# One split per FFN weight tile on ACT and DVE, and one sum of the seven products by an adding transfer

## The chip, the core and the metric

The kernel runs on one core of one Trainium2 chip. A core has five engines that each work through their own queue in order and wait for each other by semaphores: PE multiplies matrices, DVE and ACT work elementwise, POOL does small elementwise work and issues transfers, and SP issues transfers. The metric is the device time of one execution in microseconds. The time before is 1067.16 us, the median of three runs from 1063.83 to 1067.43.

## What is computed

One decoder layer for 256 tokens and 16 meta tokens with 2048 channels, in float32. After attention, pooling and a first normalisation comes the part that the change touches, a gated FFN with a causal convolution of width 3, and a second normalisation:

```python
def conv_gated_ffn(h, w_up, conv_w, conv_b, w_down):
    T = h.shape[1]
    z = h @ w_up
    zp = jnp.pad(z, ((0, 0), (CONV_WIDTH - 1, 0), (0, 0)))
    z = sum(zp[:, j:j + T] * conv_w[j] for j in range(CONV_WIDTH)) + conv_b
    a, g = jnp.split(z, 2, axis=-1)
    return (jax.nn.gelu(a) * g) @ w_down
...
        f = conv_gated_ffn(h, w_up[l], conv_w[l], conv_b[l], w_down[l])
        h = layer_norm(ALPHA * h + f, ln2_g[l], ln2_b[l])
```

`w_up` is 2048 by 11264, `w_down` 5632 by 2048.

## The kernel before

**Two parts for each number.** PE multiplies rounded float32 values (fp32r). To keep float32 precision, each operand is split into a high part (the value rounded) and a low part (the rest), and each product is three matmuls: high by high, high by low, low by high (L172 to L174 in `product`, L742 to L744 in `seven`). For weights the split is made on the chip as they arrive, in `fetch`: SP issues the transfer of a 128 x 2048 tile into a raw buffer `wraw` (L108), ACT copies it to the high half of `whl` (L121), and DVE writes raw minus high into the low half (L122). Raw and split buffers both come three deep, so a transfer waits until the L122 of three tiles earlier has ended, and a split waits until PE has done with the tile three earlier. `weights()` asks for a tile, and with it for the next two.

**Up tiles and down tiles.** An up tile is one block of 128 output channels of `w_up`: 48 matmuls of 258 columns. Its result goes through the convolution on ACT and DVE (L680 to L682), and for each second up tile the gate (L697, L698). Two gated blocks make a pair, which is turned into the left-hand forms of a seven-product scheme for 2 x 2 blocks: sums on POOL (`forms`, L717 to L720), their high and low parts on ACT and DVE (`two_parts`, L703 and L704).

A down tile holds the four blocks b11, b12, b21, b22 of 512 columns that belong to one pair and one half c of the output. Of kind A, it serves four products (P2, P3, P1, P5), after DVE has put b12 - b11 in the place of b12 (L113). Of kind B, it serves three (P7, P6, P4), after DVE has made three differences and sums in place (L116, L117, L118, which write b12, b11 and b21 in this order); then only 1536 columns are split. The products of one part and one half c are summed over the part's pairs in PSUM; four pairs (three in parts of 6) make an A phase, and then as many tiles of kind B a B phase.

**The order.** The 44 channel blocks come in parts of 8, 8, 8, 8, 6 and 6 (`PARTS`). `ffn_plan` lays the up tiles of one part between the down tiles of the part before it, in even shares: one to one as long as the parts are equal, four down tiles to three up tiles while the fifth part goes up and the fourth comes down. The last part's down projection is done plainly at the end. The first four blocks (`FOLDED`) are multiplied before the first normalisation is known, and put right afterwards by `unfold`; these are the first eight up tiles. The order on each engine is not that of the source: a scheduler in the framework arranges the instructions of all engines from its own estimate of their times when the kernel is built.

**The sums.** At the end of an A phase ACT copies P1 and P5 to `u` and `v` (L754, L756), DVE adds P2 and P3 to the output blocks c11 and c12 in `y2` (`add`, L750), and POOL issues two transfers that add `u` to c11 and `v` to c12 in place (L759, L760). At the end of a B phase DVE adds `v` (still P5) to c22, `u` becomes P1 + P6 (L764), `v` becomes `u` + P7 (L765), P4 goes to c21, and three more adding transfers bring `u` to c12 and `v` to c21 and c22. In the first part `add` also multiplies the block by ALPHA.

The two lines that say how a tile is cut:

```python
        cuts = (0, 1024, 2048)
...
            cuts = (0, 1024, 1536)
```

Of the kernel before, what the change touches and what calls it, by code (L numbers as in the profile page):

```python
# [14 lines left out]
ALU = mybir.AluOpType  # L15
# [53 lines left out]
def tile_layer(ctx, tc, xt, w_first, w_proj, w_uk, w_uv, w_pool, w_o, w_up, w_down, cols, rows, rel_bias, onehot, out):  # L69
    nc = tc.nc  # L70
# [10 lines left out]
    def small():  # L81
        return pa.tile([P, 512], F32, tag="at", name="at")
# [9 lines left out]
    stream = [w_proj[j] for j in range(8)] + [w_uk, w_uv] + [w_proj[j] for j in range(8, 24)]  # L92
    stream += [w_o[j] for j in range(KT)]
    plan = ffn_plan()
    kinds = {}
    for item in plan:
        if item[0] == "up":
            stream.append(w_up[item[2] * FT + item[1]])
        else:
            kinds[len(stream)] = item[0]  # L100
            stream.append(w_down[sum(PARTS[:item[1]]) + item[2] * (PARTS[item[1]] // 2) + item[3]])
    stream += [w_down[d] for d in range(FT - PARTS[-1], FT)]
    spare, scattered = len(stream) - PARTS[-1], (len(stream) - 2, len(stream) - 1)
# [3 lines left out]
    def fetch(raw, hl, src, kind=None):  # L107
        nc.sync.dma_start(raw, src)  # L108
        b11, b12, b21, b22 = (raw[:, c:c + 512] for c in range(0, 2048, 512))
        cuts = (0, 1024, 2048)  # L110
        if kind == "A":

            nc.vector.tensor_tensor(b12, b12, b11, op=ALU.subtract)  # L113
        if kind == "B":

            nc.vector.tensor_tensor(b12, b22, b12, op=ALU.subtract)  # L116
            nc.vector.tensor_tensor(b11, b12, b11, op=ALU.add)  # L117
            nc.vector.tensor_tensor(b21, b21, b11, op=ALU.subtract)  # L118
            cuts = (0, 1024, 1536)
        for c in (slice(a, b) for a, b in zip(cuts, cuts[1:])):  # L120
            nc.scalar.activation(hl[:, 0, c], raw[:, c], AF.Copy)  # L121
            nc.vector.tensor_tensor(hl[:, 1, c], raw[:, c], hl[:, 0, c].bitcast(F32), op=ALU.subtract)  # L122
# [4 lines left out]
    def emit(i):  # L127
        if i in ready:
            return
        if i in scattered:  # L130

            raw = wp.tile([P, 2048], F32, tag="wraw", name="wraw")
            nc.sync.dma_start(raw, stream[i])
            ready[i] = []
            for c in range(0, 2048, 256):
                hl = ring.tile([P, 2, 256], F32R, tag="act", name="whl_r", padded_shape=[P, 2, T])
                nc.scalar.activation(hl[:, 0, :], raw[:, c:c + 256], AF.Copy)
                nc.vector.tensor_tensor(hl[:, 1, :], raw[:, c:c + 256], hl[:, 0, :].bitcast(F32), op=ALU.subtract)
                ready[i].append(hl)
            return  # L140
        if i == spare:
            raw = wp.tile([P, 2048], F32, tag="wraw", name="wraw")
            hl = sb.tile([P, 2, 2048], F32R, tag="y", name="whl_y")
        else:
            raw, hl = weight_tiles()
        fetch(raw, hl, stream[i], kinds.get(i))
        ready[i] = hl
# [6 lines left out]
    def weights(ahead=2):  # L154
        i = state["use"]
        state["use"] += 1
        prefetch(i + 1 + ahead)
        return ready.pop(i)
# [113 lines left out]
    cuts = ((0, P), (P, 2 * P), (2 * P, T))  # L272
    v = sb.tile([P, 3], F32, name="rms_v")
# [103 lines left out]
    for i, (a, b) in enumerate(((0, NM), (NM, NM + P), (NM + P, T))):  # L377
        if i:
            v = ap_.tile([b - a, 1024], F32, name=f"v{i}")
        else:  # L380

            v = ap_.tile([80, 1024], F32R, name="v0")
# [248 lines left out]
    cuts = ((0, P), (P, 2 * P), (2 * P, NQ))  # L631
# [68 lines left out]
    held = {}  # L700
# [30 lines left out]
    def seven(kind, part, c, j):  # L731

        hl = weights()
        n = PARTS[part] // 2
        names = (("P2", 2), ("P3", 3), ("P1", 0), ("P5", 1)) if kind == "A" else (("P7", 1), ("P6", 0), ("P4", 2))
        if j == 0:
            for name, _ in names:
                held[name] = small()
        for name, w in names:
            a, i = pairs[part][j][name]  # L740
            ps, w = held[name], slice(512 * w, 512 * w + 512)
            nc.tensor.matmul(ps, a[:, 0, i], hl[:, 0, w], start=j == 0, stop=False)  # L742
            nc.tensor.matmul(ps, a[:, 0, i], hl[:, 1, w], start=False, stop=False)  # L743
            nc.tensor.matmul(ps, a[:, 1, i], hl[:, 0, w], start=False, stop=j == n - 1)  # L744
        if j < n - 1:
            return
        c11, c12, c21, c22 = (y2[:, i, w:w + 512] for i in range(2) for w in (512 * c, 1024 + 512 * c))

        def add(to, ps):
            nc.vector.scalar_tensor_tensor(to, to, 1.0 if part else ALPHA, ps, op0=ALU.mult, op1=ALU.add)  # L750

        if kind == "A":
            held["u"] = fp.tile([P, 512], F32, name="u", tag="u1", bufs=1, padded_shape=[P, 2 * NQ])
            nc.scalar.activation(held["u"], held["P1"], AF.Copy)  # L754
            held["v"] = fp.tile([P, 512], F32, name="v", tag="u2", bufs=1, padded_shape=[P, 2 * NQ])
            nc.scalar.activation(held["v"], held["P5"], AF.Copy)  # L756
            add(c11, held["P2"])
            add(c12, held["P3"])
            nc.gpsimd.dma_start(c11, held["u"], accum_op=ALU.add)  # L759
            nc.gpsimd.dma_start(c12, held["v"], accum_op=ALU.add)  # L760
        else:
            u, v = held["u"], held["v"]
            add(c22, v)
            nc.vector.tensor_tensor(u, u, held["P6"], op=ALU.add)  # L764
            nc.vector.tensor_tensor(v, u, held["P7"], op=ALU.add)  # L765
            add(c21, held["P4"])
            nc.gpsimd.dma_start(c12, u, accum_op=ALU.add)
            nc.gpsimd.dma_start(c21, v, accum_op=ALU.add)
            nc.gpsimd.dma_start(c22, v, accum_op=ALU.add)
# [4 lines left out]
    for item in plan:  # L774
        if item[0] in "AB":
            seven(*item)
            continue
        _, f, half_ = item
        part = next(p for p in range(len(PARTS)) if f < sum(PARTS[:p + 1]))
# [161 lines left out]
```

## Time and profile before

| | us |
|---|---|
| median of three runs | 1067.16 |
| lowest, highest | 1063.83, 1067.43 |
| the profiled execution | 1061.57 |
| its span, first to last instruction | 1059.8 |

How to read the rows. A page row of an engine gives its busy time, its share of the span and its instructions. PE's weight loads (PEld) overlap its matmuls, and matmuls overlap each other, so the pace of PE is read from starts. A row of stretches gives the stretch, its length and each engine's busy time in it with the number of instructions, then the clock that PE was granted, the mean busy share of the 16 DMA engines, and GB/s. A row of waits gives who waited for whom, the total in us, the times and the longest. A row of a group gives line, engine, operation, out<-in, shapes and count, then busy us and the mean ns of one, then the idle time of the engine just before them and what ended it. A row of the timeline gives start and length in us, the engine, line and operation, and x4 where four equal ones follow each other. Line numbers are those of the kernel before.

### The profile page before, as it was taken

How to read it: one execution, taken by the hardware profiler on the slowest of the kernel's cores; microseconds unless marked ns; L12 is line 12 of the kernel's file. 1: busy time of each engine (PE TensorE's matmuls, PEld its weight loads, DVE VectorE, ACT ScalarE, POOL GpSimd, SP SyncE). 2: the span in 40 equal slices, each digit the busy share in tenths (PEclk: the TensorE clock that was granted, in tenths of full speed). 3: DMA queues.
4: the chain of work that ended last, by engine and by line, in shares of the span. 5: the costliest groups of instructions: out<-in, count | busy, mean ns of one | idle time of the engine just before them, and what ended most of it. 6: DMA issues, size and time to landing. Idle time of an engine off the chain costs nothing. (4 is left out here: it accounts for less than half of the span.)

```text
span 1059.8 us, 19247 instructions
## 1 busy us (share of the span) xinstructions
PE 1040.1 (98%) x7683; PEld 989.0 (93%) x7683; DVE 902.1 (85%) x1391; ACT 605.1 (57%) x968; POOL 207.0 (20%) x257
## 2 busy tenths in 40 slices
PE   9999999999999999999999999999999998999996
PEld 8998999999999999999999999999999897999985
DVE  6879468848769987899899989899898999998977
ACT  6566445745447765565565656565565555665650
POOL 1100014125345321210112101122011212200020
PEclk9999999999999999999999999999999999999998
DMA  8756542454552577898787797877878787898882
GB/s 319 255 172 238 192 148 96 158 184 168 181 190 93 187 228 233 276 292 279 270 292 271 267 298 268 280 262 273 296 272 271 260 288 262 286 300 300 298 272 80
DMA packets 60330, 253.16 MB, mean 239 GB/s; under 512 B 21798, under 2 KB 22224, under 8 KB 32976
## 3 DMA queue, kind: packets, MB, share of 16 engines
q1 hardware_dynamic: 34448, 231.86, 60.3%
q0 software_dynamic: 8320, 16.93, 8.4%
q10 hardware_dynamic: 17472, 3.15, 1.6%
q8 instruction: 60, 0.98, 0.4%
q14 instruction: 30, 0.25, 0.1%
HBM read 234.60 MB, written 2.11 MB: 223 GB/s over the span
## 5 line engine op out<-in xcount | busy, mean ns | idle before, releaser
L122 DVE TENSOR_TENSOR whl<-wraw,whl 128x1024 fp32r<-128x1024 f32 (+1 forms) x418 | 491.0, 1210 | 53.2 <-ACT whl L121 51.1
L121 ACT ACTIVATE whl<-wraw 128x1024 fp32r<-128x1024 f32 (+1 forms) x418 | 403.5, 1012 | 133.9 <-DVE wraw L113 28.9
L172 PE MATMUL mm<-hp,whl 128*128 128x258 f32 x1280 | 364.6, 285 | 0.2 <-ACT whl L121 0.2
L174 PE MATMUL mm<-hp,whl 128*128 128x258 f32 x1280 | 361.9, 283 | 1.5 <-DVE whl L122 1.5
L173 PE MATMUL mm<-hp,whl 128*128 128x258 f32 x1280 | 362.6, 283 | 0.0
L173 PEld LDWEIGHTS mm<-hp,whl 128*128 128x128 f32 x1280 | 244.3, 191 | 3.1
L174 PEld LDWEIGHTS mm<-hp,whl 128*128 128x128 f32 x1280 | 243.8, 190 | 1.9 <-DVE whl L122 1.9
L172 PEld LDWEIGHTS mm<-hp,whl 128*128 128x128 f32 x1280 | 242.1, 189 | 3.5 <-ACT whl L121 0.4
L172 PE MATMUL mm<-xp,whl 128*128 128x256 f32 (+5 forms) x384 | 111.0, 289 | 0.0
L173 PE MATMUL mm<-xp,whl 128*128 128x256 f32 (+5 forms) x384 | 109.5, 285 | 0.0
L174 PE MATMUL mm<-xp,whl 128*128 128x256 f32 (+5 forms) x384 | 109.1, 284 | 0.3 <-DVE whl L122 0.3
L742 PE MATMUL at<-whl,gp 128*128 128x512 f32 x190 | 75.2, 396 | 0.0
L743 PE MATMUL at<-whl,gp 128*128 128x512 f32 x190 | 74.9, 394 | 0.0
L744 PE MATMUL at<-whl,gp 128*128 128x512 f32 x190 | 74.8, 394 | 0.0
L172 PEld LDWEIGHTS mm<-xp,whl 128*128 128x128 f32 x384 | 72.7, 189 | 0.6
L174 PEld LDWEIGHTS mm<-xp,whl 128*128 128x128 f32 x384 | 72.5, 189 | 0.8 <-DVE whl L122 0.8
L173 PEld LDWEIGHTS mm<-xp,whl 128*128 128x128 f32 x384 | 72.3, 188 | 0.8 <-issue 0.5
L680 ACT ACTIVATE z<-mm,cv 128x256 f32<-128x256 f32 x40 | 22.5, 561 | 79.0 <-PE mm L174 78.1
L720 POOL TENSOR_TENSOR forms<-za 128x128 f32<-128x128 f32 x19 | 18.4, 967 | 207.4 <-DVE za L698 199.9
L680 ACT ACTIVATE za<-mm,cv 128x256 f32<-128x256 f32 x40 | 22.5, 562 | 56.1 <-PE mm L174 56.1
L717 POOL TENSOR_TENSOR forms<-za 128x128 f32<-128x128 f32 x19 | 21.5, 1130 | 126.4 <-DVE za L698 126.3
L744 PEld LDWEIGHTS at<-whl,gp 128*128 128x128 f32 x190 | 35.7, 188 | 8.6
(299 smaller groups left out, 1927.5 us busy)
## 6 DMA issues: line engine op xcount, KB each, us to landing
wraw<-in_w_up SPq DMA_DIRECT2D x88, 1024.0 KB, 5.3
wraw<-in_w_down SPq DMA_DIRECT2D x82, 1024.0 KB, 6.1
wraw<-in_w_proj SPq DMA_DIRECT2D x24, 1024.0 KB, 4.9
wraw<-in_w_o SPq DMA_DIRECT2D x16, 1024.0 KB, 4.8
y<-v POOLq DMA_DIRECT2D x30, 256.0 KB, 8.4
y<-u POOLq DMA_DIRECT2D x20, 256.0 KB, 4.4
wraw<-in_w_first SPq DMA_DIRECT2D x9, 304.0 KB, 5.5
x<-in_xt SPq DMA_DIRECT2D x1, 2176.0 KB, 8.4
```

The source lines that it names most:

```text
L121: nc.scalar.activation(hl[:, 0, c], raw[:, c], AF.Copy)
L122: nc.vector.tensor_tensor(hl[:, 1, c], raw[:, c], hl[:, 0, c].bitcast(F32), op=ALU.subtract)
L172: nc.tensor.matmul(ps, wh, ah, start=n == 0, stop=False)
L173: nc.tensor.matmul(ps, wh, al, start=False, stop=False)
L174: nc.tensor.matmul(ps, wl, ah, start=False, stop=n == KT - 1)
L680: nc.scalar.activation(z, src[:, 2:NQ], AF.Identity, bias=col(C_B, j), scale=col(C_W, 3 * j + 2))
L717: nc.gpsimd.tensor_tensor(s[:, 0], a21, a22, op=ALU.add)
L720: nc.gpsimd.tensor_tensor(s[:, 3], a11, a21, op=ALU.subtract)
L742: nc.tensor.matmul(ps, a[:, 0, i], hl[:, 0, w], start=j == 0, stop=False)
L743: nc.tensor.matmul(ps, a[:, 0, i], hl[:, 1, w], start=False, stop=False)
L744: nc.tensor.matmul(ps, a[:, 1, i], hl[:, 0, w], start=False, stop=j == n - 1)
```

## The change

`kinds` now also holds the up tiles, under "up", so that `fetch` sees a kind for every tile of the FFN but the last six. With a kind, a tile is cut in one piece: 2048 columns for up tiles and kind A, 1536 for kind B. Tiles without a kind (the projections, `w_o`, and the last six of `w_down`) keep their two pieces. Further, in all parts but the first, the addition of P5 to c22 moves from DVE at the end of the B phase to an adding transfer from `v` that POOL issues at the end of the A phase.

```diff
@@ -94,10 +94,10 @@
     for item in plan:
+        kinds[len(stream)] = item[0]
         if item[0] == "up":
             stream.append(w_up[item[2] * FT + item[1]])
         else:
-            kinds[len(stream)] = item[0]
             stream.append(w_down[sum(PARTS[:item[1]]) + item[2] * (PARTS[item[1]] // 2) + item[3]])
@@ -107,7 +107,7 @@
-        cuts = (0, 1024, 2048)
+        cuts = (0, 2048) if kind else (0, 1024, 2048)
         if kind == "A":
@@ -116,7 +116,7 @@
             nc.vector.tensor_tensor(b21, b21, b11, op=ALU.subtract)
-            cuts = (0, 1024, 1536)
+            cuts = (0, 1536)
@@ -758,9 +758,12 @@
             nc.gpsimd.dma_start(c11, held["u"], accum_op=ALU.add)
             nc.gpsimd.dma_start(c12, held["v"], accum_op=ALU.add)
+            if part:
+                nc.gpsimd.dma_start(c22, held["v"], accum_op=ALU.add)
         else:
             u, v = held["u"], held["v"]
-            add(c22, v)
+            if part == 0:
+                add(c22, v)
```

## The prediction

> **What bounds the kernel now.** I read the page's busy shares first, then the stretches by stage, then who waited for whom on PE.
>
> ```profile
> span 1059.8 us, 19247 instructions
> PE 1040.1 (98%) x7683; PEld 989.0 (93%) x7683; DVE 902.1 (85%) x1391; ACT 605.1 (57%) x968; POOL 207.0 (20%) x257
> ```
> ```profile
> core 0: us, PE busy (x) PEld busy (x) DVE busy (x) ACT busy (x) POOL busy (x), PEclk, DMA share, GB/s
> 283.00:412.00 129.00, 127.33 (x1046) 125.79 (x1046) 110.52 (x187) 79.19 (x132) 47.02 (x49) 1.00 0.55 180
> 412.00:570.00 158.00, 158.00 (x1121) 148.93 (x1120) 142.78 (x193) 93.17 (x129) 24.46 (x30) 1.00 0.85 279
> 570.00:821.00 251.00, 251.00 (x1774) 236.34 (x1773) 227.40 (x314) 149.31 (x208) 42.88 (x51) 1.00 0.81 275
> 821.00:915.00 94.00, 90.45 (x616) 83.23 (x615) 86.71 (x118) 53.75 (x74) 16.14 (x16) 1.00 0.81 269
> 915.00:1012.00 97.00, 97.00 (x696) 91.79 (x695) 91.71 (x126) 58.80 (x81) 10.99 (x13) 1.00 0.89 298
> ```
> ```profile
> PE mm L174 <- DVE whl L122: 2.2, 4, 0.8
> PE at L742 <- ACT whl L121: 2.0, 1, 2.0
> PE at L743 <- DVE whl L122: 0.8, 1, 0.8
> ```
> The FFN runs from 283 to 1012. TensorE sets its pace: it is busy for the whole of three of the five stretches, at a granted clock of 1.00. It loses 129 - 127.33 = 1.67 us while the first tiles run on unnormalised input, and 94 - 90.45 = 3.55 us in 821:915, where each up tile meets more down tiles. So 5.2 us is nearly all that any relief of DVE or ACT can give back here, and 0.5% of the time (5.3 us, about what a measurement can tell from no change) is as much. DVE is close behind PE: 227.40 of 251 us (91%), 86.71 of 94 (92%). The question is not how much work is taken off DVE and ACT but whether each tile is still ready when PE comes for it.
>
> **The change part by part: the pieces.** Durations by form, then one pair of tiles (an up tile and a kind-B down tile) on DVE, PE and ACT:
>
> ```profile
> L122 DVE TENSOR_TENSOR whl<-wraw,whl 128x1024 fp32r<-128x1024 f32 x380 | 468.6, 1262 | 53.2 <-ACT whl L121 51.1 <-PE at L485 0.8 <-PE at L530 0.8
> L121 ACT ACTIVATE whl<-wraw 128x1024 fp32r<-128x1024 f32 x380 | 384.8, 1051 | 133.9 <-DVE wraw L113 28.9 <-DVE wraw L117 27.5 <-issue 26.5
> L121 ACT ACTIVATE whl<-wraw 128x512 fp32r<-128x512 f32 x38 | 23.4, 616 | 0.0
> L750 DVE SCALAR_TENSOR_TENSOR y<-y,v 128x512 f32<-128x512 f32 x10 | 7.0, 699 | 0.6 <-issue 0.6
> ```
> ```profile
> 643.18 0.41 DVE L704 TENSOR_TENSOR gp<-za,gp 128x256 fp32r<-128x256 f32 x1
> ...
> 644.38 0.68 DVE L116 TENSOR_TENSOR wraw<-wraw 128x512 f32<-128x512 f32 x1
> ...
> 647.84 4.10 DVE L122 TENSOR_TENSOR whl<-wraw,whl 128x1024 fp32r<-128x1024 f32 x4 [0.18 <-ACT whl L121]
> 651.86 0.69 DVE L116 TENSOR_TENSOR wraw<-wraw 128x512 f32<-128x512 f32 x1
> 652.58 0.69 DVE L117 TENSOR_TENSOR wraw<-wraw 128x512 f32<-128x512 f32 x1
> 653.19 0.48 DVE L681 SCALAR_TENSOR_TENSOR z<-mm,cv,z 128x256 f32<-128x256 f32 x1
> 653.58 0.68 DVE L118 TENSOR_TENSOR wraw<-wraw 128x512 f32<-128x512 f32 x1
> 654.18 0.48 DVE L682 SCALAR_TENSOR_TENSOR z<-mm,cv,z 128x256 f32<-128x256 f32 x1
> 654.57 1.22 DVE L122 TENSOR_TENSOR whl<-wraw,whl 128x1024 fp32r<-128x1024 f32 x1
> 655.71 0.42 DVE L698 TENSOR_TENSOR za<-za,z 128x256 f32<-128x256 f32 x1
> 656.04 3.22 DVE L122 TENSOR_TENSOR whl<-wraw,whl 128x512 fp32r<-128x512 f32 x3
> 659.19 0.68 DVE L116 TENSOR_TENSOR wraw<-wraw 128x512 f32<-128x512 f32 x1
> ```
> ```profile
> 652.03 0.40 PE L742 MATMUL at<-whl,right 128*128 128x512 f32 x1
> 652.27 0.39 PE L743 MATMUL at<-whl,right 128*128 128x512 f32 x1
> 659.90 0.41 PE L742 MATMUL at<-whl,right 128*128 128x512 f32 x1
> ```
> ```profile
> 637.84 0.60 ACT L754 ACTIVATE u<-at 128x512 f32<-128x512 f32 x1
> 638.54 0.60 ACT L756 ACTIVATE v<-at 128x512 f32<-128x512 f32 x1
> ...
> 646.75 3.48 ACT L121 ACTIVATE whl<-wraw 128x1024 fp32r<-128x1024 f32 x4 [1.84 <-DVE wraw L117]
> 653.35 1.58 ACT L121 ACTIVATE whl<-wraw 128x1024 fp32r<-128x1024 f32 x2 [0.55 <-DVE wraw L117]
> ```
> The pace of one split is told by starts, not durations, since neighbours overlap: 1024 columns take 655.71 - 654.57 = 1.14 us on DVE, a 512 operation 0.60 where the next doesn't depend on it (653.58 to 654.18). The next 512 columns therefore cost 0.54, and one split costs 1.68 for 1536 columns and 2.22 for 2048, against 1.74 and 2.28 in two pieces: 0.06 us saved. With 88 up tiles and 76 down tiles that is 164 x 0.06 = 9.8 us off DVE. On ACT, 512 columns cost 1051 - 616 = 435 ns, so one piece takes 1.49 (1536) or 1.92 (2048).
>
> [...]
>
> **The adding transfer.** Eight of the ten additions `add(c22, v)` (all but the first part's two) leave DVE: 8 x 0.60 = 4.8 us. Each becomes one more transfer of 256 KB from POOL's queue, beside the 30 of `v` that are there:
>
> ```profile
> y<-v POOLq DMA_DIRECT2D x30, 256.0 KB, 8.4
> L760 POOL DMA_DIRECT2D y<-v x10 | 9.0, 898 | 6.6 <-issue 3.3 <-ACT whl L121 3.3
> DMA to landing us min/median/max: 4.8/5.1/7.7
> ```
> POOL issues it in 0.9 us, ahead of the other two, and the order in the built program places some of L718 to L720 (`forms`) behind all three; ACT and DVE have L703 and L704 of those forms in their own order, so up to 0.9 us of lateness can reach the next split. The transfer lands 8.4 us after issue; the next writer of `v` (L765) comes a whole B phase, about 31 us, later, and that hides it. I take 0 for it, with 0 to 0.9 us eight times as the range.
>
> **The lost pipelining.** Before, a B tile's first 1024 columns start on ACT as L117 ends (653.35, beside 652.58 + 0.69), while DVE does L118; DVE then goes on without idling. A pair costs DVE 659.19 - 651.86 = 7.33 us and PE 659.90 - 652.03 = 7.87: DVE gains 0.54 us a pair, and the B tile that PE starts at 659.90 was ready at 656.04 + 0.69 = 656.73, 3.2 us early. After, the one piece covers b21, so ACT cannot start before L118 has ended, and DVE cannot start L122 before ACT has done all 1536 columns. The built program puts nothing else between L118 and L122 but L698 in every second pair. From L118's start to L122's that is 0.69 + 0.08 (653.27 to 653.35) + 1.49 + about 0.05 = 2.30 us, where before it was 0.99. The order there is L116 of the next B tile, L122 up, L681, L117, L682, L118, L122: 0.60 + 2.22 + 0.40 + 0.60 + 0.40 + 2.30 + 1.68 = 8.20 us, 0.33 more than PE takes. Four pairs make a phase, which also holds the four L704 (644.38 - 643.18 = 1.20 us): 34.0 against PE's 31.5. What PE had in hand at the start of the phase pays first. There ACT now queues the copies u and v (L754, L756), which wait for PE's last A products, ahead of the first B split. From L756 on (638.54) that is 0.49 + 1.49 + 0.05 + 1.76 = 3.8 us until the B tile is ready, and L116 and L122 of the up tile behind it make it 6.6. PE has one up tile to do meanwhile, then the B tile: nine products of 0.24 (652.27 - 652.03) are 2.1 us, so the up tile is 5.8, and PE wants the two at 5.8 and 7.9. 1.3 us in hand: 2.5 - 1.3 = 1.2 us of PE idle a phase.
>
> Beside it stands a transfer: L116 of the next B tile needs the raw buffer that the previous up tile's L122 frees, and comes 0.40 + 0.60 + 0.40 + 2.30 + 1.68 = 5.4 us after it; landing took 4.8 to 7.7 us in this stretch. Twice a phase that is 0 to 2.3 us of DVE, with L122 of the up tile queued behind. I take 0.2 each, since 5.4 lies nearest to the median of 5.1: 1.6 us a phase in all, bounds 0 (where PE's lead takes it) and 3.5 (one of the two waits in full). At the end of a phase the built program also puts the next A tile's first product (L742) behind the up tile's first two matmuls. PE waits there for that tile's ACT split, some 0.5 + 1.92 us behind the up tile's own, while the up tile's DVE split takes 2.3 anyway: 0, at most 0.2.
>
> In A phases (one operation on the raw tile, PE needing 0.7 us more a pair) the same sum leaves about 1 us a pair over, and PE's lead comes back.
>
> **The first tiles.**
>
> ```profile
> 338.46 1.99 ACT L121 ACTIVATE whl<-wraw 128x1024 fp32r<-128x1024 f32 x2
> 339.73 2.35 DVE L122 TENSOR_TENSOR whl<-wraw,whl 128x1024 fp32r<-128x1024 f32 x2
> 341.00 0.39 PE L174 MATMUL mm<-fold,whl 128*128 128x260 f32 x1 [0.35 <-DVE whl L122]
> ```
> Here PE starts on a half and waits 0.35 us. With one piece DVE starts at 338.46 + 1.92 + 0.05 = 340.43 and ends near 342.7: PE waits 2.0. Three tiles stand like this one (second halves of pairs); the others gain, since ACT's second half no longer stands behind an instruction that waits for PE. I take 3 us, bounds 0 and 6.
>
> **The sum.** Six B phases before 821: 6 x 1.6 = 9.6. Two in 821:915, where PE already loses 3.55: followed tile by tile in the built order with the durations above, it would lose some 3.2 in the first and 2.1 in the second, since 28 merged tiles and two additions less give DVE 2.9 us back and the exposed ACT waits take more: 5.3 - 3.5 = 1.8, bounds -3.5 and 6. Two short phases after 915, with 3 pairs each: 1.6 together, bounds 0 and 5. First tiles 3. Sum 16 us, bounds -3.5 (-5 with the first tiles' 1.67 back) and 38. The profiled execution took 1061.6 us (its span 1059.8 and 1.8 around it): 1078. The median of the three runs shown is 1067.2, 5.6 higher, and the changed kernel will be measured beside such runs: 1067 + 16 = 1083 us.
>
> **The rivals.** (1) The lead of PE takes it all. Before, the B tile above was ready 3.2 us early; if ACT's single piece costs a little less than 1.49 us, or DVE's chain 0.33 less, no B phase falls short: 1067, give or take 4. For it: PE is 100% busy in 412:821. Against: 8.20 against 7.87 comes from starts in the same stretch.
> (2) Faster. In 821:915 DVE's work is what PE waits for (three waits of L742, L743 and L174 above); if ACT runs ahead, so that L122 finds its input done, the 2.9 us off DVE and the shorter ACT take back the 3.55, and with the first tiles' 1.67 the time is 1067 - 5 = 1062 us. It decides as soon as a pair costs DVE under 7.87 us. [...] Against: L121 of a B tile cannot run ahead of its own L118.
> (3) The transfers decide. If L116 waits 2 us in most pairs, phases lose 3.5 us and the late stages with them: 1067 + 30 = 1097. For it: 7.7 us landings, DMA share 0.81 to 0.89. Against: DVE's longer cycle spreads the issues, too.
>
> **How the numbers follow.** Forecast (16 us, its own range 1073 to 1094): 0.5. Rival 1: 0.2, rival 2: 0.1, rival 3: 0.2. Slower by over 0.5% holds for the forecast and rival 3: 0.7; within 0.5%: 0.2; faster: 0.1. The range 1062 to 1102 leaves out about 1 in 10 on each side.
>
> **What would show it.** L122's idle time put down to ACT's L121 (51.1 us before) should grow by 1.3 us for each of 38 B tiles, to about 100. PE's idle in 412:821 should go from 0 to some 10 us, at up and B tiles late in B phases, waiting for L122. DVE's busy time should fall by about 14 us. If PE stays without idle there, the pair's sum is wrong; if L113 and L116 show long waits for DMA, rival 3 is right; if L122 waits no longer than before, rival 2.

## The result and the profile after

The changed kernel takes 1106.01 us, the median of four runs from 1100.58 to 1107.64, beside 1065.68 us for the kernel before in the same comparison. The ratio is 1.037 (95% interval 1.0327 to 1.0412): 40 us slower, where 16 were forecast and 1102 was the upper end of the range. Direction and place were as forecast, the size was 2.5 times as large.

From the page of the changed kernel, its span and the busy times of the engines:

```profile
span 1104.7 us, 18915 instructions
PE 1058.0 (96%) x7683; PEld 996.6 (90%) x7683; DVE 883.6 (80%) x1219; ACT 591.1 (54%) x804; POOL 209.0 (19%) x265
```

DVE does 18.5 us less and the kernel takes 45 us of span more. The same four stretches of the FFN, cut where PE starts the same tiles, show where: first in the kernel before, then in the changed one (first tiles; parts of equal size; four down tiles to three up tiles; the short phases).

```profile
307.70:414.90 107.20, 105.53 (x854) 103.46 (x853) 93.94 (x169) 69.65 (x121) 39.51 (x43) 1.00 0.57 182
414.90:818.90 404.00, 404.00 (x2870) 381.20 (x2869) 366.53 (x501) 240.02 (x332) 65.97 (x78) 1.00 0.82 277
818.90:923.60 104.70, 101.15 (x686) 93.01 (x685) 97.41 (x132) 60.87 (x85) 21.11 (x22) 1.00 0.82 277
923.60:1011.70 88.10, 88.10 (x634) 83.47 (x633) 82.81 (x114) 52.73 (x70) 6.03 (x7) 1.00 0.89 293
```
```profile
309.20:422.40 113.20, 107.30 (x854) 105.00 (x854) 94.15 (x154) 69.25 (x104) 44.78 (x43) 0.98 0.54 174
422.40:848.10 425.70, 412.73 (x2870) 383.20 (x2869) 355.89 (x397) 230.14 (x232) 61.52 (x82) 1.00 0.80 264
848.10:959.70 111.60, 104.55 (x686) 94.09 (x685) 93.68 (x103) 57.19 (x56) 18.67 (x24) 0.98 0.81 269
959.70:1056.30 96.60, 91.44 (x635) 85.11 (x634) 77.93 (x88) 51.63 (x51) 8.54 (x11) 0.98 0.82 262
```

The stretches are 6.0, 21.7, 6.9 and 8.5 us longer, with the same matmuls in them. PE, which had no idle at all in the second and the fourth, now has 425.70 - 412.73 = 13.0 and 5.2 us of it, and in three of the rows its granted clock is 0.98. The idle understates the loss: the matmuls of an up tile are 0.28 us long but start 0.12 us apart, so each gap there hides another 0.16 us. The waits of the changed kernel say for whom PE and DVE stood still (total, times, longest):

```profile
DVE whl L122 <- ACT whl L121: 124.3, 104, 3.5
PE mm L174 <- DVE whl L122: 19.9, 18, 3.4
PE at L743 <- DVE whl L122: 5.2, 9, 1.1
DVE wraw L116 <- DMA wraw<-in_w_down: 9.1, 7, 2.8
DVE wraw L113 <- DMA wraw<-in_w_down: 3.0, 3, 1.3
```

### The profile page after: what moved, and what is told of

Its sections match the earlier page's. It is cut to its first block, busy times and chain, and to the rows that moved or that the text cites. A ratio compares the mean times of both kernels' runs of the same rounds, so it can differ in the third digit from the quotient of the medians.

```text
span 1104.7 us, 18915 instructions
## 1 busy us (share of the span) xinstructions
PE 1058.0 (96%) x7683; PEld 996.6 (90%) x7683; DVE 883.6 (80%) x1219; ACT 591.1 (54%) x804; POOL 209.0 (19%) x265
## 4 chain that ended last, share of the span: by engine, by line
PE 45%; DVE 25%; DMA 9%; issue 8%; ACT 8%; POOL 3%; ACTq 0%; SPq 0%; POOLq 0%; DVEq 0%
DVE whl L122 13%; PE mm L174 11%; PE mm L173 11%; PE mm L172 11%; DMA wraw<-in_w_down 7%; ACT whl L121 7%; DMA wraw<-in_w_up 2%; PE at L743 1%; PE at L742 1%; PE at L744 1%; DVE wraw L116 1%; DVE wraw L113 1%; DVE wraw L117 1%; DVE x L663 1%; DVE za L681 1%
## 5 line engine op out<-in xcount | busy, mean ns | idle before, releaser
L122 DVE TENSOR_TENSOR whl<-wraw,whl 128x2048 fp32r<-128x2048 f32 (+2 forms) x254 | 472.8, 1878 | 125.8 <-ACT whl L121 124.3
L121 ACT ACTIVATE whl<-wraw 128x2048 fp32r<-128x2048 f32 (+2 forms) x254 | 384.4, 1543 | 171.9 <-DVE wraw L113 44.6
L174 PE MATMUL mm<-hp,whl 128*128 128x258 f32 x1280 | 366.7, 286 | 18.1 <-DVE whl L122 17.9
L174 PEld LDWEIGHTS mm<-hp,whl 128*128 128x128 f32 x1280 | 246.4, 192 | 23.0 <-DVE whl L122 22.8
L173 PEld LDWEIGHTS mm<-hp,whl 128*128 128x128 f32 x1280 | 246.8, 193 | 3.0
L172 PEld LDWEIGHTS mm<-hp,whl 128*128 128x128 f32 x1280 | 244.8, 191 | 5.2 <-ACT whl L121 1.9
L742 PE MATMUL at<-whl,gp 128*128 128x512 f32 x190 | 75.1, 401 | 2.8 <-ACT whl L121 2.1
L743 PEld LDWEIGHTS at<-whl,gp 128*128 128x128 f32 x190 | 35.8, 188 | 13.0 <-DVE whl L122 6.3
L770 POOL DMA_DIRECT2D y<-u x10 | 8.8, 876 | 203.6 <-DVE u L767 203.6
L720 POOL TENSOR_TENSOR forms<-za 128x128 f32<-128x128 f32 x19 | 12.7, 666 | 181.7 <-DVE za L698 175.8
L742 PEld LDWEIGHTS at<-whl,gp 128*128 128x128 f32 x190 | 35.5, 188 | 12.0 <-ACT whl L121 5.4
```

The costliest lines, as they stand in the source:

```text
L172: nc.tensor.matmul(ps, wh, ah, start=n == 0, stop=False)
L173: nc.tensor.matmul(ps, wh, al, start=False, stop=False)
L174: nc.tensor.matmul(ps, wl, ah, start=False, stop=n == KT - 1)
L720: nc.gpsimd.tensor_tensor(s[:, 3], a11, a21, op=ALU.subtract)
```

## The experiments

All times are medians beside the kernel before on the same chip (1064.5 to 1066.2 us); each ratio has its 95% interval. Where the loss lies is told in one table at the end of this part, from the starts of PE's tiles. Lines that add `kinds` for up tiles are left out of the diffs.

### The parts of the change alone

e1 has the pieces without the moved addition, e2 the moved addition without the pieces.

```diff
@@ e1 @@
-        cuts = (0, 1024, 2048)
+        cuts = (0, 2048) if kind else (0, 1024, 2048)
...
-            cuts = (0, 1024, 1536)
+            cuts = (0, 1536)
@@ e2 @@
+            if part:
+                nc.gpsimd.dma_start(c22, held["v"], accum_op=ALU.add)
...
-            add(c22, v)
+            if part == 0:
+                add(c22, v)
```

> The one-piece cuts alone, the addition of P5 back on DVE. Theory A (the cuts cost everything, the adding transfer nothing): 40 us slower than before, 1106, or 2 to 5 us above the changed kernel's 1106, since DVE has eight additions (4.8 us) more. Theory B (POOL's third transfer makes the forms and with them DVE's chain late): 25 to 32 us slower, 1091 to 1098.

> The adding transfer alone, all tiles in two pieces. Theory A: within 3 us of before, or up to 4 us faster, as the stretch where PE lost 3.55 us has two additions less. Theory B: 8 to 15 us slower, 1074 to 1081.

e1: 1096.60 us, 1.0302 (1.0258 to 1.0346). e2: 1071.24 us, 1.0055 (1.0031 to 1.0079). The pieces make 31 of the 40 us; the transfer, which the forecast put at zero, makes 5.9 alone and 9.4 on top of the pieces. e1 lies in theory B's range, e2 in neither. Of the 9.6 us that e2's profile is longer, up to 6.8 are PE at half clock (a granted clock of 0.50; the profile's mean is 0.99, before 0.997; table, and last section).

e3 has the one piece in up tiles and kind A only, e4 in kind B only.

```diff
@@ e3 @@
-        cuts = (0, 1024, 2048)
+        cuts = (0, 2048) if kind else (0, 1024, 2048)
@@ e4 @@
-            cuts = (0, 1024, 1536)
+            cuts = (0, 1536)
```

> Up tiles and kind A in one piece, kind B in two, no transfer moved. Theory C (kind B's single piece behind L118 is what makes DVE's chain longer than PE's): 8 to 15 us slower, most of it in the first tiles; L122 idle for ACT near 75 us. Theory D (PE waits for whole up tiles, whatever B does): 25 to 32 us slower.

> Kind B alone in one piece of 1536 columns, up tiles and kind A in two, no transfer moved. Theory C: 20 to 28 us slower, all of it after the first down tile; L122 idle for ACT near 90 us. Theory D: 5 to 10 us slower.

e3: 1085.61 us, 1.0194 (1.0158 to 1.0231). e4: 1085.98 us, 1.0190 (1.0147 to 1.0233). Neither theory alone holds: e4 lies in theory C's range, e3 between the two. In the parts of equal size the two lose 6.4 and 7.7 us alone but 18.1 together (e1). Without the stretch from 440 to 480 us, where single events fall (below), it is 4.2 and 1.0 alone and 14.6 together: each alone is nearly covered by PE's lead, both together are not. Of e4's 7.7 us, 6.6 are one event, in its timeline on DVE:

```profile
449.44 0.68 DVE L118 TENSOR_TENSOR wraw<-wraw 128x512 f32<-128x512 f32 x1
450.03 0.48 DVE L682 SCALAR_TENSOR_TENSOR za<-mm,cv,za 128x256 f32<-128x256 f32 x1
456.24 0.69 DVE L116 TENSOR_TENSOR wraw<-wraw 128x512 f32<-128x512 f32 x1 [5.73 <-DMA wraw<-in_w_down]
456.85 4.02 DVE L122 TENSOR_TENSOR whl<-wraw,whl 128x1536 fp32r<-128x1536 f32 x3
```

The built order has put L116 of the next B tile ahead of L122 of this one. ACT was done with this one at 451.7; L116 waits for its transfer until 456.24, and all splits behind it wait too.

### Which engine's piece

e5 merges ACT's pieces only, ahead of the loop over the cuts, which is left with DVE's; e6 merges DVE's only, behind the loop, which is left with ACT's.

```diff
+        whole = slice(0, cuts[-1])
@@ e5 @@
+            nc.scalar.activation(hl[:, 0, whole], raw[:, whole], AF.Copy)
@@ e6 @@
+            nc.vector.tensor_tensor(hl[:, 1, whole], raw[:, whole], hl[:, 0, whole].bitcast(F32), op=ALU.subtract)
```

> Every up and down tile of the FFN is one instruction on ACT and two on DVE; the additions stay as before. Theory G (what costs is that DVE cannot begin before ACT has done the whole tile): about as slow as the cuts alone, +25 to +31 us on the kernel before, and L122 waits some 115 us for L121 in sum (119 with both cuts merged, 51 before). Theory H (what costs is that PE cannot begin a tile before the whole of L122 has ended): +0 to +10 us, and the waits of L174 and L743 for L122 stay near 3 us (20 with both merged).

> Every up and down tile of the FFN is two instructions on ACT and one on DVE; the additions stay as before. In up and A tiles DVE waits for all of ACT as with both merged, in B tiles only the last 512 columns of ACT come after L118. Theory C (the single ACT piece behind L118 sets the loss, as the prediction had it): 38 x 0.9 = 34 us less waiting of L122 for L121 than with both merged, so some 85 us, and +8 to +15 us on the kernel before. Theory H (PE waits for whole DVE pieces): +25 to +31 us, as with both merged.

e5: 1094.24 us, 1.0273 (1.0241 to 1.0305), with the low halves' instruction (L122) waiting 121 us for ACT in sum. e6: 1080.07 us, 1.0140 (1.0096 to 1.0185), and 84 us. Theories G and C hold: ACT's single piece alone loses 23.4 us in the parts of equal size, as much as the whole change loses there, though DVE's instructions are as many as before. That DVE's piece costs little is not shown by e6; e17 below speaks against it.

### The opposite dose, the transfer, the first tiles, the loads

e7 cuts into pieces of 512; e8 moves the addition except in the fourth part; e11 is the changed kernel with two pieces in the first twelve up tiles; e12 is the kernel before with pieces of 512 in those twelve.

```diff
@@ e7 @@
+        cuts = (0, 512, 1024, 1536, 2048) if kind else (0, 1024, 2048)
...
+            cuts = (0, 512, 1024, 1536)
@@ e8, from e2 @@
-            if part:
+            if part not in (0, 3):
...
-            if part == 0:
+            if part in (0, 3):
@@ e11 and e12 @@
+        kinds[len(stream)] = "first" if item[0] == "up" and item[1] < 6 else item[0]
@@ e11 @@
+        cuts = (0, 2048) if kind in ("up", "A") else (0, 1024, 2048)
@@ e12 @@
+        cuts = (0, 512, 1024, 1536, 2048) if kind == "first" else (0, 1024, 2048)
```

> The opposite dose: every up and down tile of the FFN in pieces of 512 columns (four, or three for kind B) on ACT and on DVE; the additions stay as before. If the number of DVE instructions decides, 252 further ones at 0.06 us are 15 us of DVE: PE's lead takes them in the parts of equal size, and the stretch with four down tiles to three up tiles, where DVE sets the pace, gives about 28 x 0.12 = 3 us more: 1066 to 1072 us. If the earliness of the pieces decides, PE's idle goes below that of before (5.7 us in gaps over 0.3 us): 1060 to 1064 us.

> Two pieces everywhere, as before; the adding transfer in place of the DVE addition in all parts but the first and the fourth (the one whose down tiles come four to three up tiles). Theory I (the transfer costs only by putting DVE's other work later where PE has no lead): within 2 us of the kernel before, no PE gap over 2 us and no stretch of half clock in 821:915 that the kernel before lacks. Theory J (the transfer costs in itself, by POOL's issue or the queue): +4 to +6 us still, as with all eight (+5.9).

> The changed kernel with two pieces again in the first twelve up tiles (up to the input tile 5), ahead of all down tiles. By the prediction's term for the first tiles 3 us come back; by the starts of PE's tiles in the profile of the changed kernel 6 us (1.5 before the third pair, 4.5 before the seventh), and 1.7 more if the stretch of half clock at 385 us goes with it: 1098 to 1100 us. The stretches behind 415 us stay as they are.

> The kernel before with four pieces of 512 in the first twelve up tiles alone, two elsewhere. If earlier pieces are what these tiles lack, PE's starts move 1.9 us ahead before 415 us, as with pieces of 512 everywhere, and nothing changes behind: 1061 to 1065 us. If that gain is lost behind it (PE then waits for the transfers or for DVE's order), no change.

e7: 1078.77 us, 1.0116 (1.0078 to 1.0155). e8: 1069.40 us, 1.0030 (1.0006 to 1.0053). e11: 1103.15 us, 1.0357 (1.0326 to 1.0387). e12: 1068.42 us, 1.0042 (1.0024 to 1.0060). Only e8 lies in an expected range, at the lower end of theory J's. e7, e11 and e12 have one thing in common. Each gains ahead of 415 us (1.4, 6.0 and 1.3 us in the table) and loses 6 to 8 us at about 460 us (the changed kernel 3.9), in an event like the one shown for e4: L116 waits 5.4 us (e12), 5.8 (e7) or 6.8 (e11) for its transfer ahead of splits of other tiles. There the transfers of the residual run beside those of the weights: in the kernel before six of them, of 64 KB each, are issued from 440 to 462 us, their queue takes 12.5% of the DMA engines there, and the engines' share is 1.02 and 1.07 from 445 to 450 and from 450 to 455 us. e12 changes nothing but tiles long done by then; the order that the build lays out downstream changed with it. For e7 that is a part of the miss only; it loses as much again in the stretch of four to three. e8 is unclear: it lost 3.4 us in the part where it changes nothing, up to half of it by the clock (below; of the two stretches of half clock in its profile one lies outside this part, at 1035 us).

e9 and e10 shorten the loads of the changed kernel and of the one before. They load the first 1024 columns of an up tile or a tile of kind A, which are split twice over, and the first 1536 of kind B. So they leave out weights and do not compute the layer; the number and the sizes of the splits stay.

```diff
+        loaded = slice(0, {"up": 1024, "A": 1024, "B": 1536}.get(kind, 2048))
+        nc.sync.dma_start(raw[:, loaded], src[:, loaded])
```

> The changed kernel, but each up and kind-A tile of the FFN is loaded by its first 1024 columns only, which are split twice over, and each kind-B tile by its first 1536 (b22 is left out: L116 takes b11 in its place); the splits keep their sizes and counts. Theory K (waits for transfers are a part of the loss: L113 and L116 wait 12.1 us for DMA in the changed kernel): these waits fall to under 2 us and the time by 8 to 14 us, to 1092 to 1098 us. Theory L (only the chain of L118, L121 and L122 costs): within 3 us of 1106.

> The kernel before with the same shorter loads (the control): up and kind-A tiles by 1024 columns, split twice over, kind-B tiles by 1536. Theories K and L both: L113 waits 14.9 us for DMA in the kernel before, but PE does not wait for it; 1061 to 1066 us.

e9: 1094.80 us, 1.0271 (1.0237 to 1.0305). e10: 1061.90 us, 0.9969 (0.9952 to 0.9986). The time falls as theory K said, 11 us against 3 in the control, but not for its reason: the waits of the down tiles' first operations for DMA grew from 12.1 to 55.3 us, though the transfers land sooner (medians of 3.8 us, not 4.9, for up tiles, and of 4.4 and 4.9, not 5.8, for down tiles of kind A and B), because the build lays 34 of these 76 operations earlier among the splits (2 later), and L122's waits for ACT fell from 124.3 to 65.8. That the transfers have a share in the loss is likely; how is not shown.

### The order on DVE

A down tile's first operation is queued behind the last L122 of the tile before it: in the changed kernel (e13), the kernel before (e14), e12 (e15) and e4 (e16). In these kernels L113 has become L114, and L116, L121 and L122 have become L118, L123 and L124.

```diff
-            nc.vector.tensor_tensor(b12, b22, b12, op=ALU.subtract)
+            with tc.issue_after(state["split"]):
+                nc.vector.tensor_tensor(b12, b22, b12, op=ALU.subtract)
...
-            nc.vector.tensor_tensor(hl[:, 1, c], raw[:, c], hl[:, 0, c].bitcast(F32), op=ALU.subtract)
+            state["split"] = nc.vector.tensor_tensor(hl[:, 1, c], raw[:, c], hl[:, 0, c].bitcast(F32), op=ALU.subtract).ins
```

> The changed kernel with one rule for the order on DVE: a down tile's first operation (L113 or L116) is queued behind the last L122 of the tile before it. Theory M (the built order, which puts L116 with its transfer still under way ahead of splits that are ready, makes a large part of the loss): L116's and L113's waits no longer hold a ready split, the gaps of PE over 1.4 us and the half-clock stretches behind them go, 1085 to 1096 us. Theory N (the pair's chain of 8.2 us and the exposed ACT split make it, whatever the order): within 5 us of 1106, or slower, since one operation less lies in DVE's wait for ACT.

> The kernel before with the same rule for the order on DVE (the control). PE's lead of 2 to 4 us in the parts of equal size takes the difference: 1062 to 1068 us by both theories; slower, if operations put ahead are what fills DVE's waits.

> Pieces of 512 in the first twelve up tiles, two pieces elsewhere, and the rule for the order on DVE. With pieces of 512 there alone, 2 us were gained ahead of 415 us and 6.3 lost at 461 us, where L116 waits 5.4 us for its transfer ahead of L122 of another tile. Theory M: that loss is gone and the gain stays, 1060 to 1064 us, faster than the kernel before. Theory N has no part in it; if the loss at 461 us stays, it is the late transfer itself that PE waits for, 1066 to 1070 us.

> Kind B alone in one piece, with the rule for the order on DVE. Without the rule this was 1086 us, with 6.6 us lost at 454 us (L116 waits 5.7 us for its transfer ahead of a ready L122), 6.1 in the second phase of 821:915. Theory M: the first goes and a part of the second, 1072 to 1079 us. Theory N: 38 B tiles with 1.3 us of exposed ACT are what costs, 1083 to 1088 us.

e13: 1111.93 us, 1.0429 (1.0409 to 1.0449). e14: 1062.06 us, 0.9966 (0.9948 to 0.9984). e15: 1061.46 us, 0.9962 (0.9947 to 0.9978). e16: 1078.00 us, 1.0122 (1.0082 to 1.0163). For the changed kernel theory N holds. Its waits with the rule:

```profile
DVE whl L124 <- ACT whl L123: 134.2, 111, 3.5
DVE wraw L114 <- DMA wraw<-in_w_down: 1.9, 2, 1.3
DVE wraw L118 <- DMA wraw<-in_w_down: 0.2, 1, 0.2
```

The waits for transfers are gone (12.1 to 2.1 us), the waits for ACT took their place, and the time is 6 us more, up to 3.4 of it half clock: as theory N said, an operation put ahead had also filled DVE's wait for ACT. Theory M holds for the single events only: with the rule, e4's loss at 454 us is gone (from 440 to 480 us of the kernel before, e16 loses 0.7 us, e4 6.6), and e12 turns from slower to faster (e15). e16's median is 8 us below e4's, in theory M's range, but the two intervals overlap, and its profile loses no less in the parts of equal size as a whole (9.3 us against 7.7), spread over the phases. e14 and e15 beat the kernel before by some 0.35%; between the two no difference is shown.

### What was left

e17 is e15 with L122 in one piece (DVE's half of the change alone); e18 is e15 with the adding transfer.

> DVE's half of the change alone, in tile order: L122 in one piece, L121 in two, the first twelve up tiles in four pieces on both, and the rule for the order on DVE. In the built order without the rule, and with the first tiles merged too, DVE's half cost 14.7 us. Theory P (DVE's whole pieces are harmless as long as ACT works in two and DVE goes tile by tile): 1060 to 1068 us. Theory Q (PE waiting for whole tiles costs by itself): 1072 to 1080 us.

> The adding transfer in place of the DVE addition (eight of ten), with the rule for the order on DVE, four pieces in the first twelve up tiles and two elsewhere; the same without the transfer is 1061.5 us. Theory R (the transfer cost 5.9 us only by the order that it led to and the half clock behind the gaps): 1060 to 1064 us. Theory S (the transfer costs by itself, by POOL's issue or by its share of the DMA engines): 1065 to 1069 us.

e17: 1086.62 us, 1.0193 (1.0166 to 1.0220), above both ranges: a whole L122 costs by itself, 10.0 us of it in the parts of equal size. e18: 1065.50 us, 1.0001 (0.9979 to 1.0022), in theory S's range: the kernel with the transfer is some 4 us slower in tile order as well. Theory S's reason is not shown, though. The profile loses nothing where the additions were taken from DVE. It loses 1.8 us more than e15's among the first tiles, long before the first moved transfer (575 us), and 2.7 behind 1011.7 us, where PE waits 2.59 us, not 1.49, for the last weight tile. PE's waits there, in e15 and then in e18 (L843 and L846 are L841 of the kernel before, L123 and L139 are L121 and L137):

```profile
381.29 0.39 PE L174 MATMUL mm<-hp,whl 128*128 128x258 f32 x1 [0.37 <-ACT whl L123]
1028.88 0.39 PE L843 MATMUL mm<-whl_r,gp 128*128 128x256 f32 x1 [1.49 <-ACT whl_r L139]
```
```profile
382.03 0.39 PE L174 MATMUL mm<-hp,whl 128*128 128x258 f32 x1 [0.98 <-ACT whl L123]
1031.36 0.39 PE L846 MATMUL mm<-whl_r,gp 128*128 128x256 f32 x1 [2.59 <-ACT whl_r L139]
```

e18's profile has two stretches of half clock, e15's one (table; mean granted clock 0.993 and 0.995). How the transfer leads to either wait, by the built order or by itself, was not tried.

The table gives, in us against the profile of the kernel before, how much later PE comes through each stretch, and how much of the sum PE's half clock can be at most (an estimate: 1.7, half of 3.41, for each stretch of 3.41 us at a granted clock of 0.50; less where PE also waits in it):

```
                        first  equal parts  4 to 3  short   rest   sum   half clock
changed kernel           6.0      21.8       6.9     8.5    1.7   44.9      6.8
e1  pieces only          4.7      18.1       8.0     3.4    1.6   35.8      1.7
e2  transfer only        0.0       0.0       7.0     0.0    2.6    9.6      6.8
e3  up, A one piece      7.5       6.4       8.1     0.2    5.1   27.3      8.5
e4  B one piece          0.0       7.7       6.5     0.1    4.9   19.2      8.5
e5  ACT one, DVE two     0.5      23.4       5.5     4.7    1.3   35.3      6.8
e6  ACT two, DVE one     3.8       6.5       2.6     3.0    3.6   19.4      5.1
e7  pieces of 512       -1.4       8.0       7.8     2.1    4.6   21.0      8.5
e8  transfer, not in 4th 0.0       0.0       3.4     0.0    4.0    7.4      3.4
e9  changed, short loads 6.2      17.8       5.8     4.7    2.6   37.1      8.5
e10 before, short loads  0.0       1.3      -0.4     0.0   -1.7   -0.8      0.0
e11 first tiles in two   0.0      25.7       9.2     8.0    0.7   43.6      6.8
e12 first tiles by 512  -1.3       6.3       1.0     0.0    0.5    6.5      1.7
e13 changed, in order    4.7      25.3       9.1     8.6    3.5   51.2     10.2
e14 before, in order     0.0       0.0       0.1     0.0    0.3    0.4      1.7
e15 e12, in order       -0.4       0.0       0.2     0.0    0.1   -0.2      1.7
e16 e4, in order         0.0       9.3       3.6     2.6    2.2   17.7      1.7
e17 DVE's half           4.1      10.0       5.4     2.0    3.5   25.0      6.8
e18 e15 with transfer    1.4       0.0      -0.6     0.0    3.2    3.9      3.4
```

The profiled execution of the kernel before was one of its light ones (1061.6 us; granted clock 1.00 up to 1052.57 us, and no matmul behind that), so most sums stand 2 to 5 us above the differences of the medians. Those of e3, e5, e7 and e9 stand 6 to 8 above, as their profiled executions were their longest; e4's stands 1 below, as its was the shortest.

## Point by point: what held and what failed

**PE bounds, DVE's busy time is no measure: right.** DVE lost 18.5 us of work (forecast 14.6), and PE waits more. The pieces alone save 902.1 - 885.1 = 17.0 us by e1's page, so a merged split saves 0.10 us of busy time, not 0.06; from start to start it takes 1.67 and 2.20 us in the lines below, where the forecast had 1.68 and 2.22.

**The chain of one pair: right.** Three pairs of a B phase on DVE in the changed kernel, then ACT's splits, POOL's sums and PE's waits there:

```profile
659.56 0.95 DVE L116 TENSOR_TENSOR wraw<-wraw 128x512 f32<-128x512 f32 x1
660.43 2.53 DVE L122 TENSOR_TENSOR whl<-wraw,whl 128x2048 fp32r<-128x2048 f32 x1
662.89 0.68 DVE L704 TENSOR_TENSOR gp<-za,gp 128x256 fp32r<-128x256 f32 x1
663.77 0.43 DVE L704 TENSOR_TENSOR gp<-forms,gp 128x256 fp32r<-128x256 f32 x1 [0.20 <-ACT gp L703]
...
664.74 0.48 DVE L681 SCALAR_TENSOR_TENSOR za<-mm,cv,za 128x256 f32<-128x256 f32 x1
...
666.13 0.68 DVE L118 TENSOR_TENSOR wraw<-wraw 128x512 f32<-128x512 f32 x1
668.42 1.76 DVE L122 TENSOR_TENSOR whl<-wraw,whl 128x1536 fp32r<-128x1536 f32 x1 [1.60 <-ACT whl L121]
670.82 0.69 DVE L116 TENSOR_TENSOR wraw<-wraw 128x512 f32<-128x512 f32 x1 [0.65 <-DMA wraw<-in_w_down]
671.43 2.28 DVE L122 TENSOR_TENSOR whl<-wraw,whl 128x2048 fp32r<-128x2048 f32 x1
673.63 0.48 DVE L681 SCALAR_TENSOR_TENSOR z<-mm,cv,z 128x256 f32<-128x256 f32 x1
...
675.02 0.68 DVE L118 TENSOR_TENSOR wraw<-wraw 128x512 f32<-128x512 f32 x1
675.62 0.42 DVE L698 TENSOR_TENSOR za<-za,z 128x256 f32<-128x256 f32 x1
677.31 1.76 DVE L122 TENSOR_TENSOR whl<-wraw,whl 128x1536 fp32r<-128x1536 f32 x1 [1.27 <-ACT whl L121]
678.98 0.68 DVE L116 TENSOR_TENSOR wraw<-wraw 128x512 f32<-128x512 f32 x1
...
688.52 0.69 DVE L113 TENSOR_TENSOR wraw<-wraw 128x512 f32<-128x512 f32 x1 [1.30 <-DMA wraw<-in_w_down]
```
```profile
666.25 0.42 ACT L697 ACTIVATE za<-za 128x256 f32<-128x256 f32 x1 [1.54 <-DVE za L682]
666.89 3.29 ACT L121 ACTIVATE whl<-wraw 128x1536 fp32r<-128x1536 f32 x2 [0.23 <-DVE wraw L118]
```
```profile
658.85 1.96 POOL L718 TENSOR_TENSOR forms<-forms,za 128x128 f32<-128x128 f32 x1
660.89 2.40 POOL L719 TENSOR_TENSOR forms<-za,forms 128x128 f32<-128x128 f32 x1
```
```profile
670.23 0.50 PE L743 MATMUL at<-whl,right 128*128 128x512 f32 x1 [0.82 <-DVE whl L122]
673.77 0.39 PE L174 MATMUL mm<-hp,whl 128*128 128x258 f32 x1 [1.19 <-DVE whl L122]
```

The undisturbed pair, from 670.82 to 678.98, takes 8.16 us; the forecast's sum was 8.20, against PE's 7.87. From L118's start to L122's it is 2.29 us in each of the pairs, where the forecast had 2.30.

**The price of a phase: the step that failed.** The mechanism is the forecast's; its size is not. The forecast took 1.6 us of PE idle for each of the six B phases before 821, 9.6 in all, and nothing for the A phases between them, where PE's lead was to come back. By the starts of PE's tiles the six B phases lost 4.1, 2.4, 1.8, 4.3, 2.3 and 2.0 us, 16.9 in all and 2.8 each (up to 1.7 of the first is half clock), and the A phases the other 4.9 of the 21.8. So a B phase was put at little more than half of its price, and an A phase at none.

The lines above are of the fourth of them, the dearest. In the three pairs DVE takes 688.52 - 659.56 = 28.96 us, where the forecast's terms give 3 x 8.20 + 1.20 + 2 x 0.2 = 26.2. The 2.8 us between are nearly all in three terms. The two waits for transfers were put at 0.2 each "since 5.4 lies nearest to the median of 5.1"; here they are 0.65 and 1.30, 1.55 more in sum, and the median said nothing of the late half. The four L704 take 664.74 - 662.89 = 1.85 us, not 1.20: the first takes 0.68 instead of 0.41, and the next waits 0.20 for ACT. And the first pair's L116 and L122 take 0.87 and 2.46 us from start to start, not 0.60 and 2.22. The longer L704, L116 and L122 run beside POOL's L718 and L719, which stand behind the issues of three transfers on POOL here. In the changed kernel the four L116 beside L718 and L719 take 0.95 us on average, the other 34 take 0.69; why is not shown. e1, without the added transfer, lost 2.6 us in this phase, not 4.3.

The wait of 1.60 us in two of the pairs, 1.27 in the third, is no such term: L698 fills 0.33 us of it there, and ACT's L697 ends at 666.67, before L118 does. With DVE already slower than PE, whatever PE's lead does not take of such terms is lost.

**L122's wait for ACT: the mechanism right, its reach too small.** The wait by forms:

```profile
L122 DVE TENSOR_TENSOR whl<-wraw,whl 128x2048 fp32r<-128x2048 f32 x126 | 290.1, 2317 | 48.9 <-ACT whl L121 48.8
L122 DVE TENSOR_TENSOR whl<-wraw,whl 128x1024 fp32r<-128x1024 f32 x90 | 115.1, 1305 | 34.6 <-ACT whl L121 33.6 <-PE at L530 0.8
L122 DVE TENSOR_TENSOR whl<-wraw,whl 128x1536 fp32r<-128x1536 f32 x38 | 67.7, 1781 | 42.3 <-ACT whl L121 42.0
```

The 38 B tiles wait 42.0 us, 1.1 each (1.3 forecast). The tiles outside the change wait 33.6, so of the 51.1 us before some 17.5 lay in the FFN. Up and A tiles now wait 48.8, which the forecast did not count. e5 shows that ACT's piece alone is enough for the loss in the parts of equal size, as forecast; e4 shows that B tiles alone are not enough, which the forecast did not say, and e17 that DVE's piece costs too.

**The first tiles:** 6.0 us, the upper bound, where 3 was taken; up to 1.7 of it is half clock. **821 to 915:** 6.9 us where 1.8 was taken, 0.9 above the bound of 6; up to 1.7 of it is half clock. **The short phases:** 8.5 us where 1.6 was taken, bounds 0 and 5; 3.4 us are e1's, so 5.1 came only with the transfer.

**The adding transfer: failed.** It was put at 0 and cost 5.9 us alone. The reason given, that its landing is hidden, holds as far as the next writer of `v` goes (L765, now L768, waits for no transfer; those of `v` land within 3.4 to 11.3 us); what it costs lies elsewhere: in e2 up to 6.8 of the 9.6 us are PE's half clock, in the phase above POOL's sums stand behind the issues, and in e18 the two waits are not explained. The forecast's bounds (0 to 7.2 us) were right for e2, not for the 9.4 us on top of the pieces.

**The rivals.** Rival 1 and rival 2 fell with the pair of 8.16 us. Rival 3 is right in part: L113 and L116 wait 12.1 us for DMA in the changed kernel. But 14.9 us of such waits stood before, when PE had no idle in the parts of equal size, and with these waits taken away (e13) the kernel is no faster; with 55.3 us of them and shorter loads (e9) it is 11 us faster. They are one of the things that a phase without lead pays for, not its cause.

**Left out altogether: the clock.** Up to 6.8 of the 44.9 us of span are PE running at half clock, in four stretches of 3.41 us: three stand behind gaps of 1.83, 1.83 and 2.83 us, one begins in a gap of 3.40 (last section).

## What to carry to other kernels

Where an engine feeds a bound engine through a second one (here ACT, then DVE, then PE), a merged instruction was paid twice in this kernel: in the pipelining between the two feeders (e5: 23.4 us in the parts of equal size), and in the order around them (e4: 6.6 us in one event). Compare the feeder's whole cycle, with every irregular piece of work and late transfer in it, with the bound engine's cycle; once it is longer, every such item counts as soon as the lead is used up, and single changes that the lead hides add up to more than their sum (here 6.4 and 7.7 us alone, 18.1 together). And where a build arranges the order, a change in one place can be paid far behind it (e12 changes tiles ahead of 415 us and loses 6.3 us behind, at about 460 us): look for an operation that waits for a transfer ahead of ready work, and tie it down there.

## What the runs showed of the hardware

Some gaps of PE cost more than their length here. In the changed kernel PE waits 1.83 us, until 383.49, and from 384.92 to 388.33 us its granted clock is 0.50; first PE's wait, then the three neighbouring stretches (PE's busy time and, third from the right, its clock):

```profile
383.49 0.39 PE L174 MATMUL mm<-hp,whl 128*128 128x258 f32 x1 [1.83 <-DVE whl L122]
```
```profile
381.50:384.92 3.42, 1.58 (x14) 1.43 (x12) 3.21 (x5) 1.63 (x6) 2.25 (x1) 1.00 0.29 38
384.92:388.33 3.41, 3.41 (x18) 3.41 (x17) 3.00 (x6) 3.41 (x4) 0.46 (x1) 0.50 0.87 296
388.33:391.74 3.41, 3.41 (x30) 3.41 (x30) 3.38 (x4) 1.34 (x3) 0.00 (x0) 1.00 0.69 110
```

The rows count 18 matmuls at half clock and 30 in the stretch behind. From start to start it is 0.215 us there (385.11 to 388.12 in 14 steps) and 0.12 behind it, so some 1.5 of the 3.41 us are lost. In the changed kernel's trace the granted clock is 1.00 or 0.50. While PE works there are four stretches of 0.50, each 3.41 us long, from 384.92, 466.84, 873.03 and 1050.52 us; the first two begin 81.92 us apart, 24 times 3.413 us. In the 3.42 us ahead of each PE was busy for 1.58, 1.59, 0.54 and 1.31 us. The same gap did not always cost this: the gap of 2.04 us ahead of L742 in the kernel before had no half clock behind it (granted clock 1.00 from 890.50 to 897.32 us), the same gap of 2.02 us in e14 had, from 895.80 to 899.21 us. Both kernels have a gap of 0.76 us right behind it; in e14 the two leave PE busy for 0.63 us of the 3.41 ahead of the half clock. What decides between them is not shown. The scatter of the runs goes with the clock as well: of the kernel before, the runs at a mean clock of 0.996 or more took 1061.83 to 1066.08 us, those at 0.990 or less 1069.32 to 1072.46. One took 1063.60 us at 0.995 and one 1072.46 at 0.989; 0.006 of the span is up to 6.4 of these 8.9 us.
